# Late modulation chunks multiplied on TensorE into one PSUM bank, and a half slab for the recurrence's scores

## The chip, the cores and the metric

The program runs on one core of one Trainium2 chip. TensorE (PE) multiplies; VectorE (DVE), ScalarE (ACT) and GpSimd (POOL) do the rest; SyncE (SP) issues the transfers from HBM. The metric is the device time of one execution in microseconds, the median of several runs. Each engine works through its own queue in order, and an instruction that waits for another engine holds up everything behind it in its queue.

## What is computed

Two transformer blocks on 256 tokens of width 1024. Only the beginning of the first block matters here: a modulation vector of 6 x 1024 values, computed from one conditioning vector `c`, is added and multiplied in at six places.

```python
cond = jax.nn.silu(c)
mod = cond @ w_ada[l] + b_ada[l]
sh1, sc1, g1, sh2, sc2, g2 = jnp.split(mod[:, None, :], 6, axis=-1)
h = rms_norm(x, norm1_gain[l]) * (1.0 + sc1) + sh1
proj = h @ w_in[l]
hq, hf, hi, hg, aq, ak, av, gate_h, gate_a = jnp.split(proj, split_pts, axis=-1)
y_h = hgrn2_branch(hq, hf, hi, hg, ...) @ w_hg_branch[l]
y_a = swa_branch(aq, ak, av, positions, ...) @ w_attn_branch[l]
merged = jax.nn.sigmoid(gate_h) * y_h + jax.nn.sigmoid(gate_a) * y_a
x = x + g1 * (merged @ w_out[l])
h2 = rms_norm(x, norm2_gain[l]) * (1.0 + sc2) + sh2
x = x + g2 * moe_ffn(h2, ...)        # 32 experts, 4 of them for each token
```

`sh1` and `sc1` are needed before the first projection. `g1`, `sh2`, `sc2` and `g2` are needed only after both branches. The second block has the same outline, and no modulation.

## The kernel before

Weights arrive as slabs of 128 x 4096 float32 (2 MB), ten of which fit on chip (`NSLAB`). `stream_list` fixes the order of all loads. `pump` allots a slab to the next load when fewer than ten are in use and fewer than `room` of them hold weights; the load itself starts when the previous user of that slab has finished.

`w_ada` comes in twelve chunks of 512 columns. Chunks 2, 3, 0 and 1 give `sh1` and `sc1`. `ada_mm` multiplies such a chunk on PE: eight matmuls, one for each 128 rows of `w_ada`, spread over four groups of 32 columns of the array (k and k + 4 go to the same group), each with a copy of `cond` 32 columns wide (`condr`). `ada_cols` then copies the bank out, adds up the four groups with `sel4` and turns the row into columns of `mod`.

The other eight chunks, 4 to 11, come one by one between the chunks of `w_in` (`LATE`). The first mixer (`mixer1`) runs `pieces()` through `weave`: a piece is 1024 columns of a weight slab. `prep` splits it into a rounded part (a copy on ACT, L485) and a remainder (a subtraction on DVE, L486), three pieces ahead of PE; then PE multiplies the piece in three passes, 24 matmuls of 128 x 256 (L515, L516, L517; L540 to L542 where the tokens stand in the rows). The split of a piece has four buffers, so ACT can split a piece only when PE has finished with the one four before it. There are 38 pieces of `w_in`, then 8 of the two branch projections and 8 of `w_out`.

After each piece `tick` gives one step to every running chain: the recurrence (`hgrn`, which computes its decayed scores in seven levels, each: subtract on POOL L1031 and DVE L1033, exponentiate on ACT, multiply on POOL L1041 and DVE L1042, then eight small matmuls on PE L1003, then a masked copy on DVE L1016), the attention (`swa_part`: mask and maximum on DVE, exponentials on ACT L950, division on POOL L956, transposes on PE L961), and one chain `ada_late` for each late chunk. What a step issues goes into the engines' queues behind the piece's own instructions.

`ada_late` multiplies a chunk without PE: chunks 4, 6, 8, 10 and 11 (`DV`) on DVE, eight multiply-adds of 128 x 512 (L585, L583); chunks 5, 7 and 9 with eight scalings on ACT (L588) and seven additions on POOL (L590). Two of the eight steps are issued after each piece, and the chunk's slab is free only after the last one. The four sums of a set stand in `acc`, in the slab `T` ("tmp"), which also holds the recurrence's scores `S1`, `S2` and its masks. When a set of four is complete, PE adds up the 128 rows (four matmuls with `ones`, L599), ACT copies the bank out (L603), PE turns it (four transposes, L608) and DVE adds the bias (L611). This happens twice. `T` is given back after chunk 11. PSUM has three banks for the pieces (`ps_a`) and five for everything else (`ps_b`).

Of the kernel before, what the change touches and what calls it, by code (L numbers as in the profile page):

```python
# [30 lines left out]
DV = (4, 6, 8, 10, 11)  # L31
# [192 lines left out]
class Prog:  # L224
# [4 lines left out]
    def __init__(self, tc, a, out, es):  # L229
# [25 lines left out]
        self.sel4 = cp.tile([128, 1], F32, name="sel4")  # L255
        nc.vector.memset(self.sel4, 0.0)
        for g in range(4):
            nc.vector.memset(self.sel4[32 * g:32 * g + 1], 1.0)
# [292 lines left out]
    def ada_mm(self, j):  # L551

        nc = self.nc
        w = self.load("wada", j)
        ps = self.ps("b")
# [4 lines left out]
        self.wdrop()  # L560
        return ps

    def ada_cols(self, j, ps):
# [4 lines left out]
        for t in range(4):  # L568
            nc.tensor.matmul(pm[:, t:t + 1], sb[:, t * 128:(t + 1) * 128], self.sel4, start=True, stop=True)
# [3 lines left out]
    def ada_late(self, j, w):  # L573

        nc = self.nc
        acc = self.acc[j % 4]
        if j == 8:
            yield from self.until("acc")
        for k in range(8):
            v = w[:, k * 512:(k + 1) * 512]  # L580
            if j in DV:
                if k:
                    nc.vector.scalar_tensor_tensor(acc, v, self.cond[:, k:k + 1], acc, op0=A.mult, op1=A.add)  # L583
                else:
# [12 lines left out]
        ps, = yield from self.want("b")  # L597
        for g in range(4):
            nc.tensor.matmul(ps[32 * g:32 * g + 32, :], self.ones[:, 0:32], self.acc[g], start=True, stop=True)  # L599
        self.done.add("acc")  # L600
# [9 lines left out]
        v = lambda x: x[:, 4 * j - 12:4 * j + 4].rearrange("p (g t) -> p g t", g=4)  # L610
        nc.vector.tensor_tensor(v(self.mod), pm.rearrange("p (t g r) -> p g t r", t=4, g=4)[:, :, :, 0],  # L611
                                v(self.p("b_ada")), A.add)
        self.give("b")
        self.done.add(("ada", j))
# [50 lines left out]
    def mixer1(self):  # L665
# [4 lines left out]
        HA, T = self.slab("hgA"), self.slab("tmp")  # L670
# [3 lines left out]
        self.condr = self.t("condr", 8, 32, tag="n1t", bufs=2)  # L674
        nc.vector.tensor_copy(self.condr, cond.unsqueeze(2).to_broadcast([128, 8, 32]))
# [28 lines left out]
        self.acc = [T[:, 512 * i:512 * i + 512] for i in range(4)]  # L704
        S1, S2 = _view(T, 2048, 4, 256), _view(T, 3072, 4, 128)
        hgm = T[:, 3584:3840].bitcast(U8).rearrange("p (l t) -> p l t", l=8)
# [1326 lines left out]
```

## Time and profile before

| | us |
|---|---|
| median of 3 runs (1633.61 to 1635.54) | 1635.01 |
| the profiled execution | 1633.39 |
| its span, first to last instruction | 1631.5 |
| mean granted TensorE clock | 0.957 |
| first piece of the first mixer on PE | 37.8 |
| first expert matmul (L1476) on PE | 288.4 |

A timeline row gives start, duration, engine, line, operation and operands, and in brackets how long the engine was idle before it and what ended that. A matmul in float32 stands in the trace as two records. Durations of pipelined matmuls overlap; the distance from one start to the next is what a matmul costs.

### The profile page before, as it was taken

How to read it: one execution, taken by the hardware profiler on the slowest of the kernel's cores; microseconds unless marked ns; L12 is line 12 of the kernel's file. 1: busy time of each engine (PE TensorE's matmuls, PEld its weight loads, DVE VectorE, ACT ScalarE, POOL GpSimd, SP SyncE). 2: the span in 40 equal slices, each digit the busy share in tenths (PEclk: the TensorE clock that was granted, in tenths of full speed). 3: DMA queues.
4: the chain of work that ended last, by engine and by line, in shares of the span. 5: the costliest groups of instructions: out<-in, count | busy, mean ns of one | idle time of the engine just before them, and what ended most of it. 6: DMA issues, size and time to landing. Idle time of an engine off the chain costs nothing.

```text
span 1631.5 us, 19102 instructions
## 1 busy us (share of the span) xinstructions
PE 1427.0 (87%) x8068; PEld 778.7 (48%) x8068; DVE 564.3 (35%) x1005; ACT 364.7 (22%) x596; POOL 148.8 (9%) x116
## 2 busy tenths in 40 slices
PE   5979799999899899886989899888879999897675
PEld 2969688333333323333333333333248999742232
DVE  4998785131111111211121211211145757432122
ACT  4654743101001001001001010010025554211010
POOL 0374210000000000000000000000011201000000
PEclk8989899999999999997999999999989999999888
DMA  9843387899999999998999999999995245599998
GB/s 391 340 188 134 156 356 282 328 418 428 427 428 429 426 428 429 426 428 364 428 427 428 427 428 428 426 428 427 427 429 230 95 186 227 220 419 428 427 426 333
DMA packets 43983, 591.44 MB, mean 363 GB/s; under 512 B 4817, under 2 KB 7121, under 8 KB 8049
## 3 DMA queue, kind: packets, MB, share of 16 engines
q1 hardware_dynamic: 43888, 590.12, 86.5%
q8 instruction: 67, 1.10, 0.3%
q14 instruction: 28, 0.22, 0.0%
HBM read 589.05 MB, written 1.05 MB: 362 GB/s over the span
## 4 chain that ended last, share of the span: by engine, by line
PE 27%; DMA 23%; DVE 2%; issue 1%; ACT 1%; DVEq 0%; ACTq 0%; SPq 0%
DMA slab_w<-in_wd 12%; DMA slab_w<-in_wu 7%; PE ps_a L1476 6%; DMA slab_w<-in_wgu 5%; PE ps_a L1497 4%; PE ps_a L516 2%; PE ps_a L515 2%; PE ps_a L517 2%; PE ps_b L1259 1%; PE ps_a L1938 1%; PE ps_a L1919 1%; PE ps_a L541 1%; PE ps_a L542 1%; PE ps_a L540 1%; PE ps_b L1311 1%
## 5 line engine op out<-in xcount | busy, mean ns | idle before, releaser
L1476 PE MATMUL ps_a<-slab_w,half_xg 128*64 128x512 f32 x2048 | 458.3, 598 | 6.0 <-DMA slab_w<-in_wu 6.0
L1476 PEld LDWEIGHTS ps_a<-slab_w,half_xg 128*64 128x64 f32 x2048 | 141.6, 137 | 281.5 <-issue 264.7
L1497 PE MATMUL ps_a<-slab_w,half_ac 128*64 128x512 f32 x1024 | 235.7, 601 | 3.8 <-ACT half_ac L1334 2.2
L486 DVE TENSOR_TENSOR slab_ws<-slab_w,slab_ws 128x1024 fp32r<-128x1024 f32 x110 | 152.6, 1395 | 69.3 <-ACT slab_ws L485 69.0
L515 PE MATMUL ps_a<-half_X,slab_ws 128*128 128x256 f32 x448 | 134.0, 299 | 2.9 <-ACT slab_ws L485 2.9
L485 ACT ACTIVATE slab_ws<-slab_w 128x1024 fp32r<-128x1024 f32 x110 | 115.4, 1054 | 92.7 <-PE ps_a L516 55.6
L1497 PEld LDWEIGHTS ps_a<-slab_w,half_ac 128*64 128x64 f32 x1024 | 71.2, 137 | 135.4 <-issue 129.3
L517 PE MATMUL ps_a<-half_X,slab_ws 128*128 128x256 f32 x448 | 128.8, 288 | 0.5 <-DVE slab_ws L486 0.5
L516 PE MATMUL ps_a<-half_X,slab_ws 128*128 128x256 f32 x448 | 128.7, 287 | 0.0
L1455 POOL TENSOR_TENSOR h<-h,half_ac 128x512 f32<-128x512 f32 x32 | 40.8, 1274 | 900.4 <-ACT h L1454 900.4
L1502 DVE SCALAR_TENSOR_TENSOR half_oo<-ps_a,sg,half_oo 128x512 fp32r<-128x512 f32 x32 | 24.0, 751 | 255.2 <-ACT half_oo L1501 255.2
L1453 DVE TENSOR_SCALAR half_ac<-ps_a 128x512 f32<-128x512 f32 x32 | 22.1, 692 | 220.5 <-PE ps_a L1476 220.5
L1456 DVE TENSOR_SCALAR half_ac<-ps_a 128x512 f32<-128x512 f32 x32 | 22.1, 692 | 217.2 <-PE ps_a L1476 217.2
L1919 PE MATMUL ps_a<-slab_w,half_xg 128*32 128x512 f32 x512 | 72.5, 696 | 23.5 <-DMA slab_w<-in_wgu 23.5
L515 PEld LDWEIGHTS ps_a<-half_X,slab_ws 128*128 128x128 f32 x448 | 88.1, 197 | 7.4 <-issue 4.2
L516 PEld LDWEIGHTS ps_a<-half_X,slab_ws 128*128 128x128 f32 x448 | 88.1, 197 | 1.0 <-issue 0.7
L517 PEld LDWEIGHTS ps_a<-half_X,slab_ws 128*128 128x128 f32 x448 | 87.8, 196 | 0.8 <-DVE slab_ws L486 0.8
L1454 ACT ACTIVATE h<-half_ac 128x512 f32<-128x512 f32 x32 | 20.1, 630 | 286.4 <-DVE half_ac L1453 286.4
L1501 ACT ACTIVATE half_oo<-ps_a,sg 128x512 fp32r<-128x512 f32 x32 | 22.0, 687 | 259.5 <-PE ps_a L1497 259.5
L1334 ACT ACTIVATE half_ac<-ps_b 128x512 f32<-128x512 f32 x32 | 19.1, 597 | 254.2 <-PE ps_b L1332 254.2
L1322 DVE SCALAR_TENSOR_TENSOR xT_sb<-ps_b,mod_sb,xT_sb 128x256 f32<-128x256 f32 x136 | 56.2, 476 | 20.6 <-PE ps_b L1311 20.6
L1332 PE MATMUL ps_b<-cst_sb,half_ac 128*128 128x128 f32 x128 | 21.0, 287 | 41.8 <-DVE half_ac L1457 41.8
(396 smaller groups left out, 1809.4 us busy)
## 6 DMA issues: line engine op xcount, KB each, us to landing
slab_w<-in_wu SPq DMA_DIRECT2D x128, 2048.0 KB, 29.6
slab_w<-in_wd SPq DMA_DIRECT2D x79, 2048.0 KB, 30.3
slab_w<-in_wgu SPq DMA_DIRECT2D x32, 2048.0 KB, 33.7
slab_w<-in_win SPq DMA_DIRECT2D x19, 2048.0 KB, 18.4
slab_w<-in_wada SPq DMA_DIRECT2D x12, 2048.0 KB, 8.7
slab_w<-in_wbr SPq DMA_DIRECT2D x4, 2048.0 KB, 8.0
slab_w<-in_wout SPq DMA_DIRECT2D x4, 2048.0 KB, 13.1
slab_w<-in_wd SPq DMA_DIRECT2D x2, 1024.0 KB, 36.2
```

The lines of the kernel that those rows point to most:

```text
L485: nc.scalar.activation(hi, src, AF.Copy)
L486: nc.vector.tensor_tensor(lo, src, hi.bitcast(F32), A.subtract)
L515: nc.tensor.matmul(o, H[:, c], Xh[:, k, :], start=k == 0, stop=False)
L516: nc.tensor.matmul(o, H[:, c], Xl[:, k, :], start=False, stop=False)
L517: nc.tensor.matmul(o, L[:, c], Xh[:, k, :], start=False, stop=k == nk - 1)
L1322: nc.vector.scalar_tensor_tensor(self.xT[:, dt, :], ps[:, i * 256:(i + 1) * 256], gain[:, dt:dt + 1], self.xT[:, dt, :], op0=A.mult, op1=A ...
L1453: nc.vector.tensor_scalar(act, pg, 7.0, None, A.min)
L1455: nc.gpsimd.tensor_tensor(s, s, act, A.mult)
L1476: nc.tensor.matmul(ps[64 * h:64 * h + 64, :], xg[:, k, 128 * j + 64 * h:128 * j + 64 * h + 64], w[:, h, k % 4, :], start=False, stop=k == 7)
L1497: nc.tensor.matmul(ps[64 * h:64 * h + 64, :], aT[:, k, 64 * h:64 * h + 64], w[:, h, k % 4, :], start=k == 0, stop=k == 7)
L1502: nc.vector.scalar_tensor_tensor(Ol[:, cs], ps, sg, Oh[:, cs].bitcast(F32), op0=A.mult, op1=A.subtract)
L1919: nc.tensor.matmul(ps[r, :], xg[:, k, 128 * j + 32 * h:128 * j + 32 * h + 32], w[:, h, k % 2, :], start=k == 0, stop=k == 7)
```

## The change

All eight late chunks are multiplied on PE, as the first four are, by `ada_group`. The stationary operand is `condz`, which is zero but for its column 7, where `cond` stands. A window of eight of its columns puts the chunk's result into one row r of 0 to 7 of each of the four groups of 32 rows, and adds zero to the others; so eight chunks gather in one PSUM bank, which `ada_late` holds from the first chunk to the last. It is now one chain: after each piece it looks whether a chunk has been taken from the load queue (`adaq`), and if so issues its eight matmuls at once and gives the slab back. After the last chunk the bank is copied out (ACT), four matmuls against `stk32` turn and add up the four groups in one, and two additions on DVE put the bias on. `sel4` goes (any column of `ones` serves), and so do `acc`, `DV`, the multiply-adds on DVE, the scalings on ACT and the additions on POOL. `S1`, `S2` and the masks move from a slab to a half slab (`half`, a pool of its own of four); the ten slabs have one tenant fewer, while the `room` values stay.

```diff
-DV = (4, 6, 8, 10, 11)
...
     def prep(self, pc):
         if pc.lo == 0:
             while self.q and self.q[0][0][0] == "wada":
-                self.spawn(self.ada_late(self.q[0][0][1], self.load(*self.q[0][0])), last=True)
+                key = self.q[0][0]
+                self.adaq[key[1]] = self.load(*key)
...
+    def ada_group(self, ps, j, w, r, first=True, last=True):
+        nc = self.nc
         for k in range(8):
             g = k % 4
-            nc.tensor.matmul(ps[32 * g:32 * g + 32, :], self.condr[:, k, :], w[:, k * 512:(k + 1) * 512],
-                             start=k < 4, stop=k >= 4)
+            lhs = self.condz[:, k, :] if r == 7 else self.condz[:, k, 7 - r:15 - r]
+            nc.tensor.matmul(ps[32 * g:32 * g + lhs.shape[1], :], lhs, w[:, k * 512:(k + 1) * 512],
+                             start=first and k < 4, stop=last and k >= 4, skip_group_check=not (first and last))
         self.wdrop()
...
-    def ada_late(self, j, w):
+    def ada_late(self):
         nc = self.nc
-        acc = self.acc[j % 4]
-        if j == 8:
-            yield from self.until("acc")
-        for k in range(8):
-            v = w[:, k * 512:(k + 1) * 512]
-            if j in DV:
-                if k:
-                    nc.vector.scalar_tensor_tensor(acc, v, self.cond[:, k:k + 1], acc, op0=A.mult, op1=A.add)
-                else:
-                    nc.vector.tensor_scalar(acc, v, self.cond[:, 0:1], None, A.mult)
-                yield from self.wait(k % 2)
-                continue
-            nc.scalar.activation(v if k else acc, v, AF.Copy, scale=self.cond[:, k:k + 1])
-            if k:
-                nc.gpsimd.tensor_tensor(acc, acc, v, A.add)
-            if k % 2:
+        js = sorted(LATE.values())
+        ps, = yield from self.want("b")
+        for j in js:
+            while j not in self.adaq:
                 yield
-        self.wdrop()
-        if j % 4 < 3:
-            return
-        yield 2
-        ps, = yield from self.want("b")
-        for g in range(4):
-            nc.tensor.matmul(ps[32 * g:32 * g + 32, :], self.ones[:, 0:32], self.acc[g], start=True, stop=True)
-        self.done.add("acc")
+            self.ada_group(ps, j, self.adaq.pop(j), (j - 5) % 8, j == js[0], j == js[-1])
         yield
         sb = self.t("h512", 512)
         nc.scalar.activation(sb, ps, AF.Copy)
         self.give("b")
-        yield
+        yield 2
         pm, = yield from self.want("b")
         for t in range(4):
-            nc.tensor.transpose(pm[:, t * 128:(t + 1) * 128], sb[:, t * 128:(t + 1) * 128], self.c("ident"))
+            nc.tensor.matmul(pm[:, t * 8:t * 8 + 8], sb[:, t * 128:(t + 1) * 128], self.c("stk32")[:, 0:8], start=True,
+                             stop=True)
...
-        HA, T = self.slab("hgA"), self.slab("tmp")
+        HA, T = self.slab("hgA"), self.half("tmp")
...
+        self.condz = self.t("condz", 8, 32, tag="n1t", bufs=2)
+        nc.vector.memset(self.condz, 0.0)
+        nc.vector.tensor_copy(self.condz[:, :, 7:8], cond.unsqueeze(2))
+        self.adaq = {}
...
+        self.spawn(self.ada_late(), last=True)
```

Where it moves instructions, DVE first: its queue after the recurrence's first masked copy (L1012), while chunk 6 is multiplied. `slab_w` is a weight slab, `slab_ws` a split piece, `slab_tmp` the slab T, `slab_hgA` and `slab_hgB` the recurrence's buffers. Before:

```order
L1012 COPY_PREDICATED slab_tmp<-slab_tmp,ps_b 128x512
L585 TENSOR_SCALAR slab_tmp<-slab_w,cond 128x512
L583 SCALAR_TENSOR_TENSOR slab_tmp<-slab_w,cond,slab_tmp 128x512
L486 TENSOR_TENSOR slab_ws<-slab_w,slab_ws 128x1024
L1033 TENSOR_TENSOR slab_hgB<-slab_hgA 128x512
L583 SCALAR_TENSOR_TENSOR slab_tmp<-slab_w,cond,slab_tmp 128x512 x2
L486 TENSOR_TENSOR slab_ws<-slab_w,slab_ws 128x1024
L1033 TENSOR_TENSOR slab_hgB<-slab_hgA 128x256x2
L583 SCALAR_TENSOR_TENSOR slab_tmp<-slab_w,cond,slab_tmp 128x512 x2
L486 TENSOR_TENSOR slab_ws<-slab_w,slab_ws 128x1024
L1042 TENSOR_TENSOR slab_hgB<-slab_hgB,slab_hgA 128x512
```

The same place on DVE in the changed program (line numbers are 16 or 4 lower there):

```order
L996 COPY_PREDICATED half_tmp<-half_tmp,ps_b 128x512
L482 TENSOR_TENSOR slab_ws<-slab_w,slab_ws 128x1024
L1017 TENSOR_TENSOR slab_hgB<-slab_hgA 128x512
L482 TENSOR_TENSOR slab_ws<-slab_w,slab_ws 128x1024
L1017 TENSOR_TENSOR slab_hgB<-slab_hgA 128x256x2
L482 TENSOR_TENSOR slab_ws<-slab_w,slab_ws 128x1024
L1026 TENSOR_TENSOR slab_hgB<-slab_hgB,slab_hgA 128x512
```

The multiply-adds are gone from between the splits and the recurrence's own steps; nothing takes their place.

PE, after the 20th piece of `w_in`, where eight matmuls of the recurrence's fourth level stand. Before:

```order
L517 MATMUL ps_a<-half_X,slab_ws 128x256
L1003 MATMUL ps_b<-slab_hgB 128x64 x8
L515 MATMUL ps_a<-half_X,slab_ws 128x256
L516 MATMUL ps_a<-half_X,slab_ws 128x256
L517 MATMUL ps_a<-half_X,slab_ws 128x256
```

And in the changed program:

```order
L513 MATMUL ps_a<-half_X,slab_ws 128x256
L987 MATMUL ps_b<-slab_hgB 128x64 x8
L553 MATMUL ps_b<-slab_w,condz 8x512 x8
L511 MATMUL ps_a<-half_X,slab_ws 128x256
L512 MATMUL ps_a<-half_X,slab_ws 128x256
L513 MATMUL ps_a<-half_X,slab_ws 128x256
```

The eight matmuls of chunk 8 have come in behind the recurrence's; the seven other late chunks stand in the same way after the pieces 2, 6, 12, 16, 24, 28 and 36.

SP, the loads of the middle of the first mixer, each with what it waits for (DMAHW is an earlier load, the others an engine's last use of the slab). Before:

```order
L361 DMA slab_w<-in_wada 128x4096 [waits DMAHW2_49,DVE_49]
L361 DMA slab_w<-in_win 128x4096 [waits DMAHW6_49,DMAHW1_49,Pool_49]
L361 DMA slab_w<-in_wada 128x4096 [waits DMAHW3_49,DVE_49]
L361 DMA slab_w<-in_win 128x4096 [waits DMAHW6_49,DVE_49]
L361 DMA slab_w<-in_win 128x4096 [waits DMAHW5_49,Pool_49]
L361 DMA slab_w<-in_wada 128x4096 [waits DMAHW0_49,DVE_49]
L361 DMA slab_w<-in_wbr 128x4096 [waits DMAHW7_49,DVE_49]
```

In the changed program:

```order
L356 DMA slab_w<-in_wada 128x4096 [waits DMAHW0_49,DVE_49]
L356 DMA slab_w<-in_win 128x4096 [waits DMAHW6_49,DMAHW1_49,PE_49]
L356 DMA slab_w<-in_wada 128x4096 [waits DMAHW2_49,DVE_49]
L356 DMA slab_w<-in_win 128x4096 [waits DMAHW3_49,PE_49]
L356 DMA slab_w<-in_win 128x4096 [waits DMAHW5_49,PE_49]
L356 DMA slab_w<-in_wada 128x4096 [waits DMAHW6_49,DVE_49]
L356 DMA slab_w<-in_wbr 128x4096 [waits DMAHW7_49,PE_49]
```

The loads stand in the same order. Where one waited for POOL's additions or DVE's multiply-adds on a late chunk, it now waits for PE's eight matmuls on such a chunk; the remaining waits for DVE are for the split of a piece.

## Rows read from the trace of the kernel before

**Rows 1.** The page's slices: busy tenths of 40 equal slices of the span.

```profile
PE   5979799999899899886989899888879999897675
DMA  9843387899999999998999999999995245599998
```

**Rows 2.** Stretches of the first mixer: length, then busy us by engine, clock, DMA.

```profile
36.00:74.70 38.70, 36.42 (x247) 34.61 (x248) 34.42 (x42) 26.00 (x33) 11.06 (x7) 0.89 0.83 336
74.70:134.30 59.60, 50.25 (x312) 45.57 (x310) 57.75 (x69) 30.58 (x47) 37.05 (x25) 0.86 0.49 200
134.30:184.30 50.00, 42.09 (x312) 39.51 (x309) 40.69 (x57) 28.87 (x70) 17.19 (x10) 0.90 0.31 127
184.30:288.00 103.70, 97.59 (x717) 86.39 (x715) 70.34 (x117) 46.71 (x68) 10.27 (x6) 0.97 0.74 292
```

**Rows 3.** PE's waits in 74.7 to 184.3: total us, times, longest.

```profile
PE ps_b L1003 <- DVE slab_hgB L1042: 8.5, 3, 4.3
PE ps_b L961 <- POOL slab_swA L956: 7.7, 1, 7.7
```

**Rows 4.** Stretches after PE's pauses, columns as in the other stretches.

```profile
92.80:98.80 6.00, 6.00 (x22) 5.52 (x23) 5.96 (x7) 4.73 (x8) 3.09 (x3) 0.50 0.95 366
117.80:126.00 8.20, 8.18 (x38) 8.20 (x39) 8.20 (x7) 2.49 (x3) 6.71 (x5) 0.50 0.90 361
171.00:181.00 10.00, 5.33 (x16) 3.55 (x17) 9.61 (x19) 8.54 (x25) 3.78 (x2) 0.52 0.00 1
```

**Rows 5.** PE's timeline: the eight matmuls of an early chunk.

```profile
19.30 1.92 PE L558 MATMUL ps_b<-slab_w,condr 128*32 128x512 f32 x16
```

**Rows 6.** PE's timeline where the sums of a set are added up and turned.

```profile
133.34 1.06 PE L599 MATMUL ps_b<-slab_tmp,ones 128*32 128x512 f32 x8
134.34 0.39 PE L515 MATMUL ps_a<-half_X,slab_ws 128*128 128x256 f32 x1
...
227.37 0.66 PE L608 MATMUL ps_b<-cst_sb,h 128*128 128x128 f32 x4 [0.72 <-ACT h L603]
```

**Rows 7.** Groups of instructions, 36 to 300, then DVE in 74.7 to 134.3.

```profile
L590 POOL TENSOR_TENSOR slab_tmp<-slab_tmp,slab_w 128x512 f32<-128x512 f32 x21 | 33.8, 1610 | 53.4 <-ACT slab_w L588 52.7
L583 DVE SCALAR_TENSOR_TENSOR slab_tmp<-slab_w,cond,slab_tmp 128x512 f32<-128x512 f32 x35 | 30.3, 866 | 0.7
...
L486 DVE TENSOR_TENSOR slab_ws<-slab_w,slab_ws 128x1024 fp32r<-128x1024 f32 x12 | 20.4, 1702 | 0.6 <-ACT slab_ws L485 0.6
L583 DVE SCALAR_TENSOR_TENSOR slab_tmp<-slab_w,cond,slab_tmp 128x512 f32<-128x512 f32 x7 | 5.2, 747 | 0.1
```

**Rows 8.** Timelines of DVE and POOL, the recurrence's first levels.

```profile
80.99 1.22 DVE L486 TENSOR_TENSOR slab_ws<-slab_w,slab_ws 128x1024 fp32r<-128x1024 f32 x1
99.64 3.62 POOL L590 TENSOR_TENSOR slab_tmp<-slab_tmp,slab_w 128x512 f32<-128x512 f32 x2
102.03 1.27 DVE L464 TENSOR_TENSOR tn_tt<-tn_tt,tn_rs 128x20 f32<-128x20 f32 x1
103.33 0.18 DVE L465 SCALAR_TENSOR_TENSOR tn_tt<-tn_tt,tn_rs 128x20 f32<-128x20 f32 x1
```

**Rows 9.** Timelines of POOL, SP and ACT ahead of the longest pause.

```profile
152.05 4.22 POOL L590 TENSOR_TENSOR slab_tmp<-slab_tmp,slab_w 128x512 f32<-128x512 f32 x2 [0.84 <-ACT slab_w L588]
155.16 1.47 SPq L361 DMA_DIRECT2D slab_w<-in_win  x2
165.41 1.06 ACT L485 ACTIVATE slab_ws<-slab_w 128x1024 fp32r<-128x1024 f32 x1 [12.89 <-DMA slab_w<-in_win]
```

**Rows 10.** SP's waits, and loads by kind (us to landing), 0 to 330.

```profile
SPq L361 <- DVE slab_tmp L583: 41.7, 5, 32.6
...
slab_w<-in_wada SPq DMA_DIRECT2D x12, 2048.0 KB, 8.7
```

**Rows 11.** The first block's experts, columns as in the other stretches.

```profile
300.00:740.00 440.00, 397.63 (x1872) 151.42 (x1868) 83.83 (x177) 40.04 (x71) 19.09 (x15) 0.99 1.00 426
```

**Rows 12.** Float32 matmuls over the array's full width: ns min/median/max.

```profile
L1113 PE MATMUL ps_b<-slab_hgA,ones x4: 592/828/1061, 177.2 to 189.4; 128*128 128x512 f32 x4
```

More of the change, by code (lines that the diff above doesn't have):

```diff
@@ L254, in __init__ @@
         nc.vector.memset(self.ones, 1.0)
-        self.sel4 = cp.tile([128, 1], F32, name="sel4")
-        nc.vector.memset(self.sel4, 0.0)
-        for g in range(4):
-            nc.vector.memset(self.sel4[32 * g:32 * g + 1], 1.0)
         self.eps = cp.tile([128, 1], F32, name="eps")
@@ L568, in ada_cols @@
         for t in range(4):
-            nc.tensor.matmul(pm[:, t:t + 1], sb[:, t * 128:(t + 1) * 128], self.sel4, start=True, stop=True)
+            nc.tensor.matmul(pm[:, t:t + 1], sb[:, t * 128:(t + 1) * 128], self.ones[:, 0:1], start=True, stop=True)
         s = slice(4 * j, 4 * j + 4)
         nc.vector.tensor_tensor(self.mod[:, s], pm[:, :4], self.p("b_ada")[:, s], A.add)
-    def ada_late(self, j, w):
+    def ada_late(self):
         nc = self.nc
-        acc = self.acc[j % 4]
-        if j == 8:
-            yield from self.until("acc")
-        for k in range(8):
-            v = w[:, k * 512:(k + 1) * 512]
-            if j in DV:
-                if k:
-                    nc.vector.scalar_tensor_tensor(acc, v, self.cond[:, k:k + 1], acc, op0=A.mult, op1=A.add)
-                else:
-                    nc.vector.tensor_scalar(acc, v, self.cond[:, 0:1], None, A.mult)
-                yield from self.wait(k % 2)
-                continue
-            nc.scalar.activation(v if k else acc, v, AF.Copy, scale=self.cond[:, k:k + 1])
-            if k:
-                nc.gpsimd.tensor_tensor(acc, acc, v, A.add)
-            if k % 2:
-                yield
-        self.wdrop()
-        if j % 4 < 3:
-            return
-        yield 2
-        ps, = yield from self.want("b")
-        for g in range(4):
-            nc.tensor.matmul(ps[32 * g:32 * g + 32, :], self.ones[:, 0:32], self.acc[g], start=True, stop=True)
-        self.done.add("acc")
+        js = sorted(LATE.values())
+        ps, = yield from self.want("b")
+        for j in js:
+            while j not in self.adaq:
+                yield
+            self.ada_group(ps, j, self.adaq.pop(j), (j - 5) % 8, j == js[0], j == js[-1])
         yield
@@ L604, in ada_late @@
         self.give("b")
-        yield
+        yield 2
         pm, = yield from self.want("b")
         for t in range(4):
-            nc.tensor.transpose(pm[:, t * 128:(t + 1) * 128], sb[:, t * 128:(t + 1) * 128], self.c("ident"))
+            nc.tensor.matmul(pm[:, t * 8:t * 8 + 8], sb[:, t * 128:(t + 1) * 128], self.c("stk32")[:, 0:8], start=True,
+                             stop=True)
         yield
-        v = lambda x: x[:, 4 * j - 12:4 * j + 4].rearrange("p (g t) -> p g t", g=4)
-        nc.vector.tensor_tensor(v(self.mod), pm.rearrange("p (t g r) -> p g t r", t=4, g=4)[:, :, :, 0],
-                                v(self.p("b_ada")), A.add)
+        turned = pm[:, 0:32].rearrange("p (t r) -> p t r", t=4)
+        for rs, s in ((slice(0, 7), slice(20, 48)), (slice(7, 8), slice(16, 20))):
+            v = lambda x: x[:, s].rearrange("p (r t) -> p t r", t=4)
+            nc.vector.tensor_tensor(v(self.mod), turned[:, :, rs], v(self.p("b_ada")), A.add)
         self.give("b")
-        self.done.add(("ada", j))
+        self.done.add("ada")
     def gain1p(self, name, gain, sc):
@@ L703, in mixer1 @@
         HB = self.slab("hgB")
-        self.acc = [T[:, 512 * i:512 * i + 512] for i in range(4)]
-        S1, S2 = _view(T, 2048, 4, 256), _view(T, 3072, 4, 128)
-        hgm = T[:, 3584:3840].bitcast(U8).rearrange("p (l t) -> p l t", l=8)
+        S1, S2 = _view(T, 0, 4, 256), _view(T, 1024, 4, 128)
+        hgm = T[:, 1536:1792].bitcast(U8).rearrange("p (l t) -> p l t", l=8)
         b, kk, qq = (_view(HA, 1024 * i, 4, 256) for i in range(3))
@@ L779, in pieces @@
             self.bins_open(bins)
-            yield from self.branch_pieces("wbr1", "wout1", (0, 1), bins[::-1], (("hgn", "sig"), ("swa", ("ada", 11))),
+            yield from self.branch_pieces("wbr1", "wout1", (0, 1), bins[::-1], (("hgn", "sig"), ("swa", "ada")),
                                           self.mod[:, 16:24], self.moe1_open)
@@ L1121, in hgrn_out @@
             self.done.add("hgo")
-            yield from self.until(("ada", 11))
-            self.drop()
     def route_open(self, gain, wr, w, stk):
@@ L1399, in moe1_head @@
         if self.rt is None:
-            self.done.add(("ada", 11))
             self.moe1_open()
```

8 lines of the change are left out of this document (3 added, 5 removed).

## The prediction

> **What bounds the kernel now.** I read the slices of the page first. The reader is to see two long runs in which the transfers fill nine tenths or more of every slice (the experts of the two blocks), and slices 3 to 5, some 82 to 204 us, in which they do not [rows 1]. The change lies wholly in that dip, the first mixer, 36 to 288 us. Second, I asked whether a gain there reaches the end. In the first block's experts the transfers run at a share of 1.00 and 426 GB/s [rows 11]. Nine slabs are loaded ahead, and each further load waits for PE to free a slab; so the run of transfers starts when PE reaches the first expert matmul and then has a fixed length. A microsecond won or lost before 288 us moves everything behind it by one.
>
> Third, the mixer in four stretches, A to D, by engine [rows 2]. PE is busy for 94% of A, 84% of B and C, 94% of D. B and C are where something else comes last. In B, DVE is busy for 57.75 of 59.6 us; PE waits there three times, 8.5 us in all, for L1042, the recurrence's multiplication on DVE [rows 3]. In C, PE waits once, 7.7 us, for POOL's division in the attention [rows 3]. Its cause is further back: a scaling chunk held a slab until POOL's last addition ended at 156.3 us, two loads of `w_in` went out from 155.2 us on, and ACT stood 12.89 us in front of the split of the first of them, with the attention's exponentials queued behind it [rows 9]. So both pauses go back to the late chunks, one through DVE's time, one through a slab.
>
> Fourth, what a pause costs beyond itself. After the three longer pauses the granted clock stands at 0.50 to 0.52, the lower of its two levels, 1.2 instead of 2.4 GHz, while PE works [rows 4]. Work at that level takes twice its time, so half of the busy time is lost: 3.0 us of 6.0, 4.1 of 8.2, 2.6 of 5.33. B thus loses 8.5 + 3.0 + 4.1 = 15.6 us, C 7.7 + 2.6 = 10.3. That is all there is to win on the path: 25.9 us.
>
> **What PE gains in work.** Eight chunks of eight matmuls. An early chunk of the same form took 1.92 us at the full clock [rows 5]. Eight-column operands stream the same 512 columns, and the program gives them the same tiles of 128 x 32, so I take 1.92 for each, 15.4 us in all. It can hardly be less. The most it could be is worked out below among the rivals.
>
> What a change between whole-array matmuls and tiles of 32 columns costs is seen where L599 is followed by a piece: eight records at 133.34, the next piece's first matmul 1.00 us later [rows 6]. Eight records at the pitch of the early chunk (1.92 / 16 = 0.12) are 0.96, so a change costs about 0.04 us; I take nothing. The Trainium skill, TensorEngine Tiling (Array Packing), section Tiling Modes, says that switching the tiling mode drains the engine, which speaks against scattering eight such groups among the pieces. If each of 16 changes cost a drain of the size of the matmul's tail (the 0.39 us of the record at 134.34 less 0.12 of pitch, an estimate), the sum would be 4.3 us worse; the trace does not agree, at 0.04.
>
> PE loses two additions of 1.06 us and two turns of 0.66, and at the second 0.72 us of waiting for a copy [rows 6]; it gains one new turn, also four small matmuls, which I set at 0.66. Were the old additions and turns hidden, the sum would be 3 us worse; but they stand in PE's own queue in stretches where PE is the last.
>
> **What the others lose.** DVE loses 30.3 us of multiply-adds (35, besides five first multiplications), POOL 33.8 [rows 7]; ACT loses its scalings. POOL's part counts double: a tiny DVE operation that takes 0.18 us alone took 1.27 while POOL added [rows 8], and splits that take 1.22 alone [rows 8] took 1.70 on the mean in B [rows 7]. In B alone DVE loses 5.2 us of multiply-adds [rows 7] and about 1 of a first multiplication.
>
> New waits: PE now waits for a chunk's load, with the pieces queued behind. The loads stand in the old order and land 8.7 us after issue (median) [rows 10]; a chunk is loaded ahead of the `w_in` chunk that follows it, and PE takes it two pieces before that chunk's first matmul, when ACT is already splitting the same chunk or about to. Nothing to pay unless loads were late, and they come earlier: SP's five waits for a multiply-add, 41.7 us in all [rows 10], become waits for PE. The held bank leaves four of five for the chains. In the recorded order this moves the recurrence's last steps one piece nearer to the first branch piece, about 3 us less slack; ACT and DVE have less to do there, so I take nothing, at most 3 us. The half slab, the memsets and the freed slab cost nothing that PE waits for: the `room` values still decide how many loads are ahead.
>
> **The sum, by stretch.**
> A: chunks 4 and 5, no pause to lose: +3.8.
> B: of 59.6 us, 15.6 are pauses and low clock, so 44.0 of work; less one addition (1.0), plus chunks 6, 7 and 8 (5.8): 48.8 for PE. DVE had 57.75; without multiply-adds it has 51.5, and without POOL's additions beside it some 4 less (seven of POOL's 21 additions, at their mean of 1.61 us, fall into B, 11 us, and I count a third of that): 47 to 48. The two are level, so pauses shrink and do not vanish. Bounds: none left, 48.8; all left, 64.4. I take 5 us left, a third, since DVE's surplus over PE was 13 us and is now about nought, but its steps still have to follow each other: 53.8, that is -5.8.
> C: 50.0 - 10.3 = 39.7 of work; less a turn, plus chunks 9 and 10 (3.8): 43.0. The load that ACT stood for now waits for PE's group of chunk 8, four pieces or more earlier, so the stall goes whole; 1 us for what the attention's chain may keep: 44.0, -6.0. Bounds: 43.0 and 53.3.
> D: chunk 11 +1.9, new turn +0.7, less 1.06 + 0.72 + 0.66: +0.1.
> Sum: 3.8 - 5.8 - 6.0 + 0.1 = -7.9. On the profiled execution's 1633.39 us this is 1625.5. That execution is 1.6 below the median of the runs, so I forecast 1627.1, say **1627**.
>
> **The rivals.**
> 1. DVE's steps stay last in B. The recurrence's levels follow each other through POOL, ACT, DVE and PE, one step after each piece; if this chain and not DVE's load makes the 8.5 us, they stay with their low clock: B +4.8, C -6.0, in all +2.7, 1638. For it: DVE is level with PE at best, and POOL's own recurrence steps still slow it. Against it: the splits beside POOL's work were long, and 5.2 us of multiply-adds stood right between the steps. Halfway, 1632.
> 2. Slower: PE is the bound all through, and the pauses are not the late chunks'. Then the attention's pause stays too, with another wait ending last (the exponentials behind splits that wait for PE): C +3.3. In all 3.8 + 4.8 + 3.3 + 0.1 = +12, 1647. It decides as soon as the pauses give back less than the 12 us net that PE gains in work. Against it: rows 9 name the load.
> 3. The 8-wide groups do not run side by side. A full-width float32 matmul of 512 columns shows records of 0.59 us at the least [rows 12], two a matmul; eight one after another are at most 9.5 us instead of 1.92, on seven chunks +53: 1680. Against it: same tiles as the early chunk.
> 4. All pauses go: B 48.8, C 43.0; 3.8 - 10.8 - 7.0 + 0.1 = -13.9: 1621.
>
> **How the numbers follow.** A measurement of this kernel tells 0.2% (3.3 us) from no change. The forecast with its bounds, 1620 to 1632 (rival 4 within it), gets 0.66; rival 1, 1632 to 1640, 0.20; rival 2, 0.10; rival 3, 0.03; still faster, 0.01. The range holds 8 in 10 from 1620 to 1638. Faster by more than 0.2% is below 1631.7: 0.67 (the forecast's part and 0.01); within 0.2%, up to 1638.3: 0.19; slower: 0.14 (rivals 2 and 3, and the end of rival 1).
>
> **What would show it.** In the changed kernel's profile: eight groups of matmuls from `condz`, each about 1.9 us; ACT's split no longer standing for a load near the end of `w_in`; PE's waits for L1042's successor under 4 us in all and fewer stretches at 0.50; the first expert matmul at about 280 us instead of 288.4, and the distance from there to the end unchanged. It would be wrong if PE waited for a chunk's load, if a group took more than 2.5 us, or if PE's waits for the recurrence stayed near 8 us.

## The result, and the profile after

The changed kernel takes 1615.7 us (median of 4 runs, 1612.5 to 1617.1) against 1635.3 for the kernel before: a ratio of 0.9881, interval 0.9867 to 0.9895, 19.5 us faster. The forecast was 1627, its range 1620 to 1638. The direction was right; the gain was more than twice the forecast, and lies below the range, below even the rival in which all pauses go (1621). One run of the experiments, 4875.8 us of `a_dbl`, three times the length of its nine others, is left out of its median and its ratio.

The page's slices of the changed kernel, as in [rows 1]: PE is at nine tenths or more from the second slice to the eleventh, where the third and the fifth stood at 7.

```profile
PE   5999999999989889879998998898889999897675
...
DMA  9964476999999999998999999999993255599998
```

The four stretches of the first mixer, and a stretch of the experts of the first block, columns as in [rows 2]. The borders are set at the same places in PE's work as before (the work at 37.8, 74.7, 134.3, 184.3 and 288.4 us before stands at 35.9, 76.4, 124.4, 166.3 and 268.6 now).

```profile
35.90:76.40 40.50, 40.00 (x279) 34.99 (x280) 23.70 (x31) 19.44 (x21) 0.49 (x1) 0.94 1.01 426
76.40:124.40 48.00, 47.80 (x352) 40.32 (x350) 44.40 (x60) 24.75 (x35) 23.83 (x18) 1.00 0.64 245
124.40:166.30 41.90, 41.90 (x336) 38.09 (x335) 25.41 (x43) 23.31 (x63) 6.11 (x4) 1.00 0.40 151
166.30:268.60 102.30, 97.23 (x731) 86.95 (x729) 65.84 (x106) 48.47 (x72) 8.03 (x5) 0.97 0.64 255
300.00:740.00 440.00, 393.33 (x1847) 154.84 (x1849) 80.74 (x173) 42.27 (x78) 17.81 (x14) 0.97 1.00 421
```

In B and C PE is busy for all of the time but 0.2 us, and the granted clock is 1.00 where it averaged 0.86 and 0.90. DVE still does 44.4 us of work in B's 48.0. POOL went from 37.05 to 23.8 us.

| stretch | before, us | after, us | difference | forecast |
|---|---|---|---|---|
| A, from the first piece | 36.9 | 40.5 | +3.6 | +3.8 |
| B | 59.6 | 48.0 | -11.6 | -5.8 |
| C | 50.0 | 41.9 | -8.1 | -6.0 |
| D, to the first expert matmul | 104.1 | 102.3 | -1.8 | +0.1 |
| sum | 250.6 | 232.7 | -17.9 | -7.9 |

PE's waits of the changed kernel, 35 to 215 us: everything that is left after the first pieces. [Rows 3] had 8.5 and 7.7 us here.

```profile
engine line waited for: us in total, times, longest us
PE ps_a L511 <- ACT slab_ws L481: 2.9, 1, 2.9
PE ps_a L513 <- DVE slab_ws L482: 0.5, 1, 0.5
PE ps_b L987 <- DVE slab_hgB L1026: 0.2, 1, 0.2
```

One of the eight groups of a late chunk on PE's timeline, between the recurrence's matmuls and a piece. It takes 1.90 us to the modelled end of its last matmul, and the next piece starts 1.83 us after it, as the others do (1.83 to 1.86).

```profile
110.82 1.97 PE L987 MATMUL ps_b<-slab_hgB 128*128 128x64 f32 x16 [0.20 <-DVE slab_hgB L1026]
112.72 1.90 PE L553 MATMUL ps_b<-slab_w,condz 128*8 128x512 f32 x16
114.55 0.39 PE L511 MATMUL ps_a<-half_X,slab_ws 128*128 128x256 f32 x1
```

ACT's waits of the changed kernel, 38 to 200 us, longest two: the split (L481) stands for PE to give back a split piece's buffer. The gates' copies (L816) stand for PE's products in the same way. The 12.9 us for a load [rows 9] are not there any more (one wait of 5.3 us for a load is left, at 44 us, and PE doesn't wait there); PE is what the others wait for.

```profile
ACT slab_ws L481 <- PE ps_a L512: 26.2, 12, 5.0
ACT slab_gates L816 <- PE ps_a L513: 9.3, 6, 2.3
```

From the first expert matmul (288.41 before, 268.62 now) to the span's end there are 1343.1 us before and 1346.7 after. In the second trace of the changed kernel it is 1343.6, and in all the experiments but one 1342.9 to 1344.0; the first trace of the changed kernel has 3 us more (as has one experiment's, 1347.6), 2.8 of them in the second block's mixer, which the change doesn't touch. So a microsecond before the first expert matmul is one at the end, as forecast.

### The profile page after: what moved, and what is told of

It reads as the page before. It is cut to its first block, busy times and chain, and to the rows that moved or that the text cites. A ratio compares the mean times of both kernels' runs of the same rounds, so it can differ in the third digit from the quotient of the medians.

```text
span 1615.3 us, 19222 instructions
## 1 busy us (share of the span) xinstructions
PE 1430.3 (89%) x8180; PEld 773.6 (48%) x8180; DVE 521.5 (32%) x961; ACT 350.1 (22%) x572; POOL 111.7 (7%) x95
## 4 chain that ended last, share of the span: by engine, by line
PE 27%; DMA 24%; DVE 2%; ACT 1%; issue 1%; DVEq 0%; ACTq 0%; SPq 0%
DMA slab_w<-in_wd 15%; PE ps_a L1457 6%; DMA slab_w<-in_wu 5%; DMA slab_w<-in_wgu 5%; PE ps_a L1478 5%; PE ps_a L512 2%; PE ps_a L511 2%; PE ps_a L513 2%; PE ps_b L1241 1%; PE ps_a L1900 1%; PE ps_a L537 1%; PE ps_a L536 1%; PE ps_a L538 1%; PE ps_b L1293 1%; PE ps_a L1919 1%
## 5 line engine op out<-in xcount | busy, mean ns | idle before, releaser
L482 DVE TENSOR_TENSOR slab_ws<-slab_w,slab_ws 128x1024 fp32r<-128x1024 f32 x110 | 148.3, 1354 | 93.3 <-ACT slab_ws L481 93.0
L481 ACT ACTIVATE slab_ws<-slab_w 128x1024 fp32r<-128x1024 f32 x110 | 115.5, 1054 | 99.8 <-PE ps_a L512 66.8
L511 PEld LDWEIGHTS ps_a<-half_X,slab_ws 128*128 128x128 f32 x448 | 86.7, 193 | 10.1 <-issue 5.1
L512 PEld LDWEIGHTS ps_a<-half_X,slab_ws 128*128 128x128 f32 x448 | 86.8, 194 | 1.0 <-issue 0.7
L513 PEld LDWEIGHTS ps_a<-half_X,slab_ws 128*128 128x128 f32 x448 | 86.6, 193 | 0.8 <-DVE slab_ws L482 0.8
```

What stands on the lines that cost most here:

```text
L481: nc.scalar.activation(hi, src, AF.Copy)
L482: nc.vector.tensor_tensor(lo, src, hi.bitcast(F32), A.subtract)
L511: nc.tensor.matmul(o, H[:, c], Xh[:, k, :], start=k == 0, stop=False)
L512: nc.tensor.matmul(o, H[:, c], Xl[:, k, :], start=False, stop=False)
L513: nc.tensor.matmul(o, L[:, c], Xh[:, k, :], start=False, stop=k == nk - 1)
```

## The experiments

Each experiment's length below is the stretch from the first piece of the mixer to the first piece of its output projection, read from PE's timeline: 201.6 us before, 183.8 and 184.4 in two traces of the changed kernel. It holds all late chunks, and leaves out what varies between executions on either side.

### DVE's sums, and ACT's and POOL's sums, left out of the kernel before

Theory D: the recurrence's pauses come from DVE's time and the attention's from the slab of chunk 9. Theory P: POOL's additions made both.

`b_nodve` keeps of DVE's chunks the first multiplication only:

```
-                if k:
-                    nc.vector.scalar_tensor_tensor(acc, v, self.cond[:, k:k + 1], acc, op0=A.mult, op1=A.add)
-                else:
+                if k == 0:
```

> The kernel before, with DVE's five late chunks (4, 6, 8, 10, 11) reduced to their first multiplication: 35 multiply-adds of DVE are left out, so seven eighths of the sum for these chunks is missing from the output. ACT's and POOL's three chunks, all loads and PE's order stay. Theory D (the pauses in B come from DVE's time): PE's waits for L1042 fall from 8.5 us to under 2 and the low clock behind them goes, the attention's pause of 7.7 us stays: about 15 us faster, 1620. Theory P (POOL's additions, queued between the recurrence's steps and slowing DVE, make them): the first pause, 3.4 us at 92.8, beside which DVE multiplies chunk 6, goes at most, the second, 4.3 us at 117.8, beside which ACT and POOL work on chunk 7, stays: 0 to 7 us faster, 1628 to 1635.

`b_nopool` keeps of the three others the first scaling only:

```
-            nc.scalar.activation(v if k else acc, v, AF.Copy, scale=self.cond[:, k:k + 1])
-            if k:
-                nc.gpsimd.tensor_tensor(acc, acc, v, A.add)
+            if k == 0:
+                nc.scalar.activation(acc, v, AF.Copy, scale=self.cond[:, k:k + 1])
```

> The kernel before, with ACT's and POOL's three late chunks (5, 7, 9) reduced to their first scaling: 21 scalings on ACT and 21 additions on POOL are left out, so seven eighths of the sum for these chunks is missing from the output. DVE's five chunks, all loads and PE's order stay. Theory D: the attention's pause goes (its load no longer waits for POOL's last addition on chunk 9), 7.7 us and 2.6 of low clock, the recurrence's pauses stay: about 1625. Theory P: those go too, up to 26 us in all, 1609.

Measured: `b_nodve` 1620.2 us (0.9916, 0.989 to 0.9943), the mixer's stretch 190.0; `b_nopool` 1612.0 (0.9862, 0.9837 to 0.9887), the stretch 181.7. PE's waits, 34 to 190 us, of the first:

```profile
PE ps_b L1001 <- DVE slab_hgB L1040: 5.2, 2, 2.8
...
PE ps_b L959 <- POOL slab_swA L954: 2.8, 1, 2.8
```

and of the second:

```profile
PE ps_b L1002 <- DVE slab_hgB L1041: 4.7, 4, 3.2
...
PE ps_b L960 <- POOL slab_hgB L955: 0.3, 1, 0.3
```

The recurrence's two long pauses in the kernel before:

```profile
92.80 3.65 PE L1003 MATMUL ps_b<-slab_hgB 128*128 128x64 f32 x16 [3.38 <-DVE slab_hgB L1042]
...
117.82 2.58 PE L1003 MATMUL ps_b<-slab_hgB 128*128 128x64 f32 x11 [4.29 <-DVE slab_hgB L1042]
```

Neither theory holds alone. (L1040 and L1041 are before's L1042, shifted by the edit.) Without DVE's sums the first of these pauses is gone and two of 2.8 and 2.5 us stand behind it; without ACT's and POOL's the first stays at 3.2 and the second falls from 4.3 to 0.4 and less. Each pause has its chunk beside it: chunk 6 on DVE at the first (two multiply-adds from 88.1 us on), chunk 7 on ACT and POOL at the second (two additions from 115.8). Leaving out either kind leaves more than half of the recurrence's 8.5 us (5.2 and 4.7); the changed kernel, which has neither kind and adds the groups on PE, leaves 0.2.

The attention's pause goes with the load that ACT stands for. ACT's split behind that load in the kernel before is in [rows 9], 12.89 us; in `b_nodve` and `b_nopool`:

```profile
153.86 1.06 ACT L485 ACTIVATE slab_ws<-slab_w 128x1024 fp32r<-128x1024 f32 x1 [8.75 <-DMA slab_w<-in_win]
```

```profile
141.49 1.06 ACT L485 ACTIVATE slab_ws<-slab_w 128x1024 fp32r<-128x1024 f32 x1 [3.34 <-DMA slab_w<-in_win]
```

12.9, 8.8 and 3.3 us of standing go with pauses of 7.7, 2.8 and 0.3 us on PE. The load itself was issued 10 us earlier in its trace in the one and 21 in the other (145.2 and 133.9 instead of 155.2 us), of which 3.4 and 4.1 are an earlier first piece; in the changed kernel at 114.7, and its split does not wait for it.

### The same work put back beside PE's groups

`a_slab` is the changed kernel with the scores in a whole slab; it tests the slab, and gives room for what follows.

```
-        HA, T = self.slab("hgA"), self.half("tmp")
+        HA, T = self.slab("hgA"), self.slab("tmp")
...
```

> The changed kernel with the recurrence's scores back in a whole slab instead of half a one, nothing else. If the gain is the arithmetic's, the same time within 2 us (1614 to 1618), since the room values and not the number of slabs decide how many loads are ahead. If the freed slab let loads go out earlier, part of the pauses returns: 1620 or more.

Measured: 1616.5 us (0.9886, 0.9861 to 0.9911), the stretch 184.3: the half slab does nothing here. On it, `a_dve` issues DVE's 40 operations, and `a_pool` ACT's and POOL's 45, on idle memory. The diff of `a_dve`, whose `scr` are three rows of the idle half of T; `a_pool` is alike, with the two operations of the kernel before for chunks 5, 7 and 9:

```
                 self.adaq[key[1]] = self.load(*key)
+                self.spawn(self.idle_sums(key[1]), last=True)
...
+    def idle_sums(self, j):
+        nc = self.nc
+        acc, v, t = self.scr
+        if j in (5, 7, 9):
+            return
+        for k in range(8):
+            if k:
+                nc.vector.scalar_tensor_tensor(acc, v, self.cond[:, k:k + 1], acc, op0=A.mult, op1=A.add)
+            else:
+                nc.vector.tensor_scalar(acc, v, self.cond[:, 0:1], None, A.mult)
+            yield from self.wait(k % 2)
...
```

> The changed kernel (scores in a whole slab) with DVE's 35 multiply-adds and 5 first multiplications put back beside PE's groups, at the places where the kernel before issues them, on idle memory: the result is not used and no slab is held. If DVE's time made the recurrence's pauses, DVE has 51 of 49 us to do there: a pause of 2 to 4 us and its low clock come back, 1619 to 1624. If it takes POOL's additions too, 1616 to 1618.

> The changed kernel (scores in a whole slab) with ACT's 21 scalings and POOL's 21 additions put back beside PE's groups, at the places where the kernel before issues them, on idle memory: the result is not used and no slab of weights is held for it. If the engines' time made the recurrence's pauses (POOL's queue, and DVE slowed beside POOL), they come back, 3 to 5 us and as much low clock: 1622 to 1626; the attention's pause does not, since no load waits. If holding slabs made the pauses, no change: 1616.

Measured: `a_dve` 1620.9 us (0.9913, 0.9896 to 0.9929), the stretch 189.7, 5.4 more than `a_slab`; `a_pool` 1628.0 (0.9959, 0.9946 to 0.9971), 195.9, 11.6 more, and above the 1622 to 1626 expected. PE's waits of `a_dve`, then of `a_pool`, 38 to 200 us:

```profile
PE ps_b L1002 <- DVE slab_hgB L1041: 3.0, 3, 2.1
PE ps_a L537 <- ACT slab_swA L744: 0.2, 1, 0.2
```

```profile
PE ps_b L1002 <- DVE slab_hgB L1041: 7.6, 2, 6.7
PE ps_a L537 <- ACT slab_swA L744: 0.2, 1, 0.2
```

So the engines' time alone, with no slab held, brings the recurrence's pauses back, and low clock behind the longest of them (after the 2.1 us of `a_dve`, from 94.8 us on, 6.0 us at 0.72). Here are the 6.0 us behind the longest pause of `a_pool`, with PE at work throughout at 0.50, and its stretch B as a whole, in which DVE, without a multiply-add, is busy for 54.4 us where it was for 44.4 in the changed kernel:

```profile
118.50:124.50 6.00, 6.00 (x28) 3.90 (x32) 6.00 (x4) 2.63 (x4) 5.97 (x4) 0.50 0.38 164
...
76.00:136.00 60.00, 52.27 (x353) 42.63 (x352) 54.40 (x63) 29.75 (x43) 38.38 (x25) 0.91 0.47 177
```

The attention's pause is in neither: that one needs the held slab. The size of `a_pool` is to be read as an upper one. My idle row for the scaled values is one row, so ACT's scaling waits for POOL's last addition, 2.7 and 2.8 us in the stretch ahead of the long pause, which the kernel before, scaling the chunk in place, does not have:

```profile
109.99 0.73 ACT L579 ACTIVATE slab_tmp<-slab_tmp,cond 128x512 f32<-128x512 f32 x1 [2.68 <-POOL slab_tmp L581]
...
116.98 0.72 ACT L579 ACTIVATE slab_tmp<-slab_tmp,cond 128x512 f32<-128x512 f32 x1 [2.80 <-POOL slab_tmp L581]
```

### PE's groups doubled, and left out

`a_dbl` multiplies each late chunk twice by half the vector (the halved vector lies in the idle columns of T); `a_none` multiplies chunk 4 alone and only drops the others' slabs.

```
-        for k in range(8):
-            g = k % 4
-            lhs = self.condz[:, k, :] if r == 7 else self.condz[:, k, 7 - r:15 - r]
+        cz, reps = (self.condz, 1) if first and last else (self.condh, 2)
+        for i in range(8 * reps):
+            k, g = i % 8, i % 4
+            lhs = cz[:, k, :] if r == 7 else cz[:, k, 7 - r:15 - r]
...
```

```
-            self.ada_group(ps, j, self.adaq.pop(j), (j - 5) % 8, j == js[0], j == js[-1])
+            w = self.adaq.pop(j)
+            if j == js[0]:
+                self.ada_group(ps, j, w, 7)
+            else:
+                self.wdrop()
```

> The changed kernel, each late chunk multiplied twice by half the vector: PE has 64 more matmuls, 8 times 1.84 us = 14.7 us. If PE is now last through the whole mixer, the time grows by all of it, to 1630, with no new pause. If another engine's chain stood close behind PE with slack to spare on PE, less than 10 us. If the switches between tiles and the whole array cost something, more than 16.

> The changed kernel with seven of its eight late groups left out (chunks 5 to 11 are loaded but not multiplied, so their part of the modulation is missing from the output). If PE is last through the whole mixer, 7 times 1.84 us = 12.9 us faster than the changed kernel, 1603. If DVE stands close behind (45.2 of 49.4 us busy in the recurrence's stretch, where 5.5 us of PE's work go away), pauses with their low clock come back there: 1606 to 1610.

Measured: `a_dbl` 1628.1 us (0.997, 0.9947 to 0.9994), the stretch 197.0, 13.2 more than the changed kernel's; `a_none` 1604.3 (0.9829, 0.9802 to 0.9857), 173.0, 10.8 less. A doubled group, with the piece behind it:

```profile
117.41 3.62 PE L554 MATMUL ps_b<-slab_w,half_tmp 128*8 128x512 f32 x32
120.96 0.39 PE L511 MATMUL ps_a<-half_X,slab_ws 128*128 128x256 f32 x1
```

The piece starts 3.55 us after the group (3.55 to 3.57 in all eight), so eight more matmuls cost 1.72 where a group alone costs 1.84. The 0.12 us between them I read as going to tiles of eight columns and back, 0.06 a change, 1.0 us over all eight groups. Eight times 1.72 is 13.8 us, and 13.2 (12.7 against the second trace) came: PE is last through the whole stretch. `a_none` gives back 10.8 (11.4) of 12.9, since the recurrence's waits return, here PE's, 38 to 200 us:

```profile
PE ps_b L991 <- DVE slab_hgB L1030: 2.8, 3, 2.2
```

No group after chunk 4, one and two groups to a chunk go with 2.8, 0.2 and no wait for the recurrence. So leaving out the sums takes the recurrence's 8.5 us of waits to 2.8, and PE's own work in between hides the rest. In the recurrence's stretch of `a_none` PE and DVE are level, and the granted clock is 1.00 in spite of a pause of 2.2 us:

```profile
73.00:116.00 43.00, 40.59 (x289) 37.71 (x287) 41.40 (x53) 23.19 (x32) 24.07 (x18) 1.00 0.84 356
...
105.59 1.97 PE L991 MATMUL ps_b<-slab_hgB 128*128 128x64 f32 x16 [2.21 <-DVE slab_hgB L1030]
```

The 2.2 us don't stand right behind a group that is left out: they come at the third set of the recurrence's matmuls behind the place of chunk 7's group. A group thus gives DVE a lead that can last for several pieces.

### The attention's products, side by side

D came out 1.9 us better than forecast, and the trace shows where: the six products L973 took 5.7 us before, and their successors L957 take 3.7. Before, at 192.8 to 208.1 us:

```profile
192.81 1.93 PE L973 MATMUL ps_b<-slab_swA 128*64 128x512 f32 x4
194.67 0.66 PE L961 MATMUL ps_b<-cst_sb,slab_hgB 128*128 128x128 f32 x4
...
198.13 1.93 PE L973 MATMUL ps_b<-slab_swA 128*64 128x512 f32 x4
...
203.05 1.07 PE L973 MATMUL ps_b<-slab_hgB,slab_swA 128*64 128x512 f32 x2
...
207.12 1.07 PE L973 MATMUL ps_b<-slab_hgB,slab_swA 128*64 128x512 f32 x2
```

and after:

```profile
181.38 1.94 PE L957 MATMUL ps_b<-slab_swA 128*64 128x512 f32 x8
183.15 1.02 PE L957 MATMUL ps_b<-slab_hgB,slab_swA 128*64 128x512 f32 x2
184.10 0.39 PE L511 MATMUL ps_a<-half_X,slab_ws 128*128 128x256 f32 x1
...
187.17 1.07 PE L957 MATMUL ps_b<-slab_hgB,slab_swA 128*64 128x512 f32 x2
```

(Two records to a matmul.) Two matmuls of one key head take 1.86 us to the start of what follows; four, two of either head, queued together take 1.77, with another such product behind them. The two heads use different halves of the array's columns. That the four stand in one place is in the order of the changed kernel; that the held bank brought them there, since a step of the attention must wait for a bank, was not tried. `b_pair` does the pairing alone, in the kernel before, for both token blocks:

```
-        for kb in range(tb + 1):
+        def mm(kb, g=g, pt=pt):
...
+        if g == 0:
+            mx["mm", tb] = mm
+        else:
+            while mx.get(("mm", tb)) is None:
+                yield
+            for kb in range(tb + 1):
+                mx["mm", tb](kb)
+                mm(kb)
```

> The kernel before, only with the attention's products L973 of the two key heads issued together, tile beside tile, as the changed kernel's order has the first four of them. If issuing them together is what shortened them, four take 1.8 us where they took 3.7, and the last two 1.0 instead of 2.0: 2.8 us less PE work, 1632, the pauses unchanged.

Measured: 1631.9 us (0.9983, 0.9971 to 0.9995), 2.8 us less by the ratio, as expected, with the four products in 1.87 us to the start of the next piece, where two took 1.86, and the last two in 1.01, where each took 1.0:

```profile
195.29 1.94 PE L973 MATMUL ps_b<-slab_swA 128*64 128x512 f32 x8
197.16 0.39 PE L515 MATMUL ps_a<-half_X,slab_ws 128*128 128x256 f32 x1
...
203.10 1.08 PE L973 MATMUL ps_b<-slab_hgB,slab_swA 128*64 128x512 f32 x4
```

The Trainium skill, TensorEngine Tiling (Array Packing), section Tiling Modes, says that different tiles can run matmuls in parallel; these rows agree, for matmuls that stand next to each other in PE's queue.

This trace showed one thing more. Its first piece starts at 33.66 us, 4.2 earlier than in the trace of before, but PE then waits 3.3 us for DVE in a place where the trace of before has no wait:

```profile
PE ps_b L1011 <- DVE slab_hgB L1050: 7.2, 3, 2.8
PE ps_b L1011 <- DVE slab_hgA L727: 3.3, 1, 3.3
```

so the stretch is 201.7 us, though 2.8 of PE's work are gone: the 2.8 us stand in the products' rows and in the median, not in this trace's stretch. Most of the earlier start was lost again to a wait at the recurrence; whether that goes for other executions of the kernel before, this one trace doesn't tell.

### Versions between the two

Some late chunks lie where DVE has room (A, C, D). `hyb` sums chunks 4, 10 and 11 on DVE and brings each sum into its row by one matmul (three side by side), and has the paired products. `hyb2` does it for 4 and 10, `hyb4` for 4, 5 and 10. In all three the scores lie in a whole slab again, whose other half holds the sums. The core of the diff:

```
+                if key[1] in DV:
+                    self.spawn(self.dve_sum(key[1]), last=True)
...
+        for g, j in enumerate(DV):
+            nc.tensor.matmul(ps[32 * g:32 * g + 8, :], self.onez[:, 7 - row[j]:15 - row[j]], self.acc[j], start=False,
+                             stop=True, skip_group_check=True)
...
```

> A version between the two, meant to be faster: chunks 5 to 9 on PE as in the changed kernel, chunks 4, 10 and 11, which lie where DVE is idle for a third of the time and more, summed on DVE and brought in by three matmuls side by side; the attention's last two products side by side too. PE has 3 times 1.84 less, about 1.0 more, and 0.9 less for the pair: 5.4 us less than the changed kernel. If PE is last there and DVE's work is hidden, 1610 to 1611; if chunk 10's held slab or DVE's time brings a pause back, 1616 or more.

> Chunks 4 and 10 on DVE, the six others on PE, the attention's last two products side by side. Chunk 11 is back on PE, since with it on DVE the split of a branch piece came 2.5 us late. PE has 2 times 1.84 less, about 1.0 more and 0.9 less than in the changed kernel: 3.6 us less, 1612, without a pause; 1615 or more if DVE's work brings one back.

> Chunks 4, 5 and 10 on DVE, the five others on PE, the attention's last two products side by side. PE has 3 times 1.84 less, about 1.0 more and 0.9 less than in the changed kernel: 5.4 us less, 1610, if DVE can hide two chunks, 13 us of multiply-adds, ahead of the recurrence, where it is busy 20 of 36 us; if chunk 5's multiply-adds run into the recurrence's first steps, a pause with its low clock comes back: 1614 or more.

> The changed kernel itself, beside the two versions of this call: 1615 to 1617. The time up to the first piece, 35.9 us in its first trace and 37.8 in that of the kernel before, should vary between executions by a microsecond or two if it is the clock's; the stretch from the first piece to the first output piece should be 183.8 within 0.5.

Measured: `hyb` 1612.4 us (0.9869, 0.9851 to 0.9887), above the 1610 to 1611 expected without a pause, with one new pause, a branch piece's split on DVE, behind chunk 11's sum:

```profile
PE ps_a L515 <- DVE slab_bin L485: 2.5, 1, 2.5
```

Beside each other on one chip: the changed kernel again 1615.1 (0.9885, 0.9866 to 0.9903; runs 1614.4 to 1617.2; first piece at 35.5 us, stretch 184.4), `hyb2` 1609.5 (0.9843, 0.9825 to 0.9861; 1608.1 to 1610.5), `hyb4` 1609.9 (0.9847, 0.9826 to 0.9868; 1608.0 to 1610.0). Both beat the kernel before and the changed one, whose runs they don't overlap. The stretch of `hyb2` is 180.6, 3.3 to 3.8 us less than the changed kernel's (3.6 expected); the medians are 5.6 apart, and the other 2 us are not followed. PE's waits of `hyb2`, 38 to 200 us, show no new one:

```profile
PE ps_b L1030 <- DVE slab_hgB L1069: 0.2, 1, 0.2
PE ps_a L539 <- ACT slab_swA L764: 0.2, 1, 0.2
```

`hyb4` has a stretch of 179.7, with a new wait of 1.2 us at the recurrence's first step: the third chunk on DVE earns less than a microsecond, which the times can't tell.

## Why the prediction was wrong

**What bounds the kernel.** Right: the dip of the first mixer, and one to one to the end (1342.9 to 1344.0 us behind the first expert matmul in all traces but two). The earlier start of the changed kernel's trace, 35.9 instead of 37.8 us, is a matter of executions: the other traces, of either kind, start between 33.7 and 36.1 (35.5 for the changed kernel's second), and that of before was the latest. It is not part of the -17.9. Some 1.6 us of the 19.5 in the medians are thus not followed to a place; the interval is 4.6 us wide.

**What PE gains in work.** Right to a tenth of a microsecond a group: 1.83 to 1.86, not 1.92, and A came to +3.6. A change between whole-array matmuls and tiles costs 0.06, not 0.04, in all 1.0 us and within the 1.84. The estimate of 4.3 us that I made from the drain in the Trainium skill, TensorEngine Tiling (Array Packing), section Tiling Modes, is four times the 1.0 us measured here.

**What the others lose.** Right in kind: chunks 6 and 7 each stood beside one pause, and `b_nodve` and `b_nopool` show both needed. DVE's load in B came out at 44.4 us, below the 47 to 48 that I worked out: besides its sums it lost 7.1 us, where I had taken 4 for POOL's additions going away. `a_pool`, which puts those back, has it at 54.4.

**The sum by stretch.** This is the step that failed, by two terms.
First, "I take 5 us left, a third" in B, and "1 us for what the attention's chain may keep" in C: nothing was left of either. I had PE at 48.8 and DVE at 47 to 48, called them level, and let level engines cost each other 5 us, a third of what there was; no row stood behind that 5. PE came out at 48.0, with a wait of 0.2 us, and DVE at 44.4, so the two were not level. In `a_none` they are (40.6 and 41.4 us), and even there PE waits 2.8 us and not 5, at the full clock. The groups take away the rest: a piece that is followed by a group takes 4.7 us instead of 2.9, and the other engines have that much longer. `a_none`, the changed kernel and `a_dbl` show it, with waits of 2.8, 0.2 and none. Whether it is the total of PE's work that counts or the place of the groups between the steps, these runs don't separate, since both change together. With the 0.85 us wait for ACT ahead of the first pause, which I had left out of the 8.5, B's 5.8 us of error are accounted for.
Second, D at "+0.1": the order of the changed kernel showed four of the attention's products in one place, and I didn't read it. That is 2.0 us, shown by the rows above and by `b_pair`. About 1 us in C and D together I have not followed further.
So -7.9 becomes -17.9: 5.8 in B, 1.0 and 2.0 and about 1.0 in C and D, 0.2 in A.

**The rivals and the range.** Rival 1 (the recurrence's steps stay last) got 0.20 and was wrong; `a_dve` and `a_pool` show what it would have taken, 51 us of DVE's work in 53 and 54 in 60. Rival 2 fell with the attention's pause, which is gone. Rival 4, all pauses go, was the case, and I had put it at the very edge of the range, at 1621. Its own sum lacked the pair of products and the wait for ACT, 2.9 us, so that the range ended above the time that came. Rival 3 fell with the first group of 1.90 us.

**What would show it.** All signs but one came as written: eight groups of 1.9 us, no load near the end of `w_in` that ACT stands for, under 4 us of PE's waits for the recurrence, no stretch at 0.50 in B and C. The first expert matmul came at 268.6 us, not at about 280: 10 us of that are the error of the sum, 1.9 the earlier first piece.

## What to carry to other kernels

When work is put on the engine that is last, don't count it as a cost alone: it also gives the other engines' chains that much longer, and can hide what is left of their pauses (2.8 us here, once the sums were gone; with the sums still there, in `a_dve` and `a_pool`, it could not). An engine that is busy for 92% of a stretch need not cost a wait there. Where the pauses went altogether, the low clock behind them went too, and the two together were what this change had to win (17 us of waits, some 10 of low clock, against 15 of added matmuls). Once PE is last everywhere, give back to the idle engine the chunks that lie where it has room, as `hyb2` does, and not those beside the chain.

## What the runs showed of the hardware

Sums on two engines cost more together than apart. All the pauses and the low clock behind them were about 27 us. Without DVE's sums the stretch is 11.6 us shorter, without ACT's and POOL's 19.8; so the one alone leaves about 15 of the 27 and the other about 7, 22 together (one trace each). POOL's additions lengthen what DVE does beside them: with the same work, DVE is busy for 44.4 us in B of the changed kernel and for 54.4 in that of `a_pool`. The split alone is no clean measure of it. Its mean in B was 1.70 us before [rows 7] and 1.55 in the changed kernel, but 1.77 in `b_nopool`, which leaves POOL's additions out:

```profile
L482 DVE TENSOR_TENSOR slab_ws<-slab_w,slab_ws 128x1024 fp32r<-128x1024 f32 x12 | 18.6, 1550 | 3.8 <-ACT slab_ws L481 3.7
...
L486 DVE TENSOR_TENSOR slab_ws<-slab_w,slab_ws 128x1024 fp32r<-128x1024 f32 x11 | 19.4, 1767 | 1.3 <-ACT slab_ws L485 1.3
```

Operands of 8 columns cost PE what those of 32 do (1.83 and 1.86 us a group), and products on halves of the columns ran side by side where they were neighbours in the queue, and not where they were apart (1.87 us for four in `b_pair`, 1.86 for two in the kernel before). The low clock doesn't follow every pause of PE: behind the 2.2 us of `a_none` the granted clock is 1.00, behind the 2.1 us of `a_dve` 0.72 over 6.0 us, and these runs don't show what decides. The granted clock stood at 1.00 for all of 76 to 166 us, in which PE had no pause over 0.2 us.
